# A hybrid encoder layer on one Trainium2 core: the first feed-forward product goes from eight block products to seven

## The chip, the core and the metric

The kernel runs on one core of one Trainium2 chip. Its time is the time of one execution in device microseconds; lower is better. Five engines work side by side, each on its own queue in order: PE (TensorE, the matrix products), DVE (VectorE), ACT (ScalarE), POOL (GpSimd) and SP (SyncE, which issues most DMA transfers). A profile names instructions by engine and by line of the kernel file; "L75 DVE" is a vector instruction that line 75 issued.

## The reference

The reference is one layer of a hybrid encoder over 512 tokens of 1024 features, in float32. A gated branch and an attention branch are mixed, multiplied by `w_out`, normalised and added to the input, which gives `h`. Then comes the feed-forward part:

```
mix_out = merged @ w_out
h = h + rms_norm(mix_out, norm_mix_post)
n2 = rms_norm(h, norm_mlp_pre)
hid = square(relu(n2 @ w_up))            # 512 x 1024 by 1024 x 4096
h = h + rms_norm(hid @ w_down, norm_mlp_post)
```

## The kernel before

All large products run on PE in a 32-bit format of reduced precision (`F32R`). To keep float32 accuracy each operand is split into a high part `hi` (a copy on ACT, L74 or L79) and the rest `lo` (a subtraction on DVE, L75 or L80), and each product is three matmuls: high times high, high times low, low times high (`mm3`, L82 to L86). So a product costs three matmuls with a 128x128 stationary tile and a moving tile of up to 512 columns.

The back half of the kernel, with which this case deals, has three stages.

- **`w_out` (L543 to L583).** Eight accumulators in PSUM, one for each token tile `t` (128 tokens) and half of the features, are filled over eight feature tiles `k`. The first four `k` go over all tokens; the last four (`last`, L563) are done token tile by token tile, so that one token tile ends 24 matmuls after the other. When a token tile is complete, `post_norm` (L529) takes ACT Squares of the PSUM banks (L534, into a scratch tile `junk`), multiplies by the gain on DVE (L538), computes the reciprocal root on DVE and POOL (`rstd_of`, L90, L93, L96) and adds the residual (L541). The tile `h2`, all four token tiles in one buffer, was loaded with x by one POOL DMA. Then a second norm follows: Squares of `h2` on ACT (L574, into a second `junk`), `rstd_of` again, the scaled tile `xn` on DVE (L578), eight PE transposes (L581) and the split into `n2h` and `n2l` (L583). `xn` has a single buffer.
- **`w_up` (L587 to L623).** `KF` is 32: there are 32 tiles of 128 hidden features, in 16 loaded pairs of 1 MB. The first four tiles (`NSPLIT`) are computed in two halves of 256 tokens, first tokens 0 to 255 of all four, then 256 to 511, because the second half of the tokens is normalised later. The other 28 tiles take all 512 tokens in one go: 24 matmuls of 512 columns each. `up_evac` (L601) makes relu on ACT (L604) and the product with the PSUM tile on DVE (L605), which is the square of relu. All 32 `hid` tiles stay in SBUF.
- **`w_down` (L627 to L659).** For each of the 32 hidden tiles the weights and `hid` are split, and 24 matmuls of 512 columns go into eight accumulators; the last four hidden tiles are done token tile by token tile, with `post_norm` and the output DMA behind each. `dpool`, which holds the split `hid` tiles, is opened before the pools of the `w_up` stage.

The order of the instructions in each engine's queue is set when the kernel is built: a scheduler runs a timing model of the program and writes out the queues. At run time an engine waits on semaphores at the head of its queue and nothing overtakes.

Of the kernel before, what the change touches and what calls it, by code (L numbers as in the profile page):

```python
# [10 lines left out]
F32 = mybir.dt.float32  # L11
F32R = mybir.dt.float32r
AF = mybir.ActivationFunctionType
# [23 lines left out]
def block_kernel(ctx: ExitStack, tc: tile.TileContext, x, norm_mix_pre, w_in, b_gate, ln_v_gain, ln_v_bias,  # L37
# [14 lines left out]
    wpool = pool(ctx, "wpool", bufs=3)  # L52

    ident = consts.tile([P, P], F32, name="ident")
    cols = consts.tile([P, 24], F32, name="cols")
# [366 lines left out]
    rows = gpool.tile([24, P], F32, name="rows")  # L422
    for i, (vec, n) in enumerate(((b_gate, 16), (ln_v_gain, 4), (ln_v_bias, 4))):
        o = (0, 16, 20)[i]
        nc.gpsimd.dma_start(rows[o:o + n], vec[0].rearrange("(a p) -> a p", p=P))
    wsp = gpool.tile([P, 4, P], F32, name="wsp")
    nc.gpsimd.dma_start(wsp, w_spatial.rearrange("g t s -> t g s"))
    pt = psA.tile([P, 24], F32, name="ptr", tag="T")
    nc.tensor.transpose(pt, rows, ident[:24, :24])
# [84 lines left out]
    hpool = pool(back, "hpool", side="right")  # L514
    gain2 = hpool.tile([P, 3, D], F32, name="gain2")
    for i, gn in enumerate((norm_mix_post, norm_mlp_pre, norm_mlp_post)):
        nc.gpsimd.dma_start(gain2[:, i], gn.to_broadcast([P, D]))
    h2 = hpool.tile([P, 4, D], F32, name="h2")
    nc.gpsimd.dma_start(h2, x.rearrange("(t p) d -> p t d", p=P))
    n2s = ExitStack()  # L520
    n2pool = pool(n2s, "n2pool", side="right")
    n2h = n2pool.tile([P, KD, S], F32R, name="n2h")
    n2l = n2pool.tile([P, KD, S], F32R, name="n2l")
    halves = [slice(0, 512), slice(512, 1024)]

# [3 lines left out]
    def post_norm(pss, gain, yp, dst, res):  # L529
        ss = small.tile([P, 2], F32, name="ss2")  # L530
        ys = []
        for hf, hs in enumerate(halves):
            junk = yp.tile([P, 512], F32, name="junk", bufs=1)
            nc.scalar.activation(junk, pss[hf], AF.Square, accum_out=ss[:, hf:hf + 1])  # L534
# [29 lines left out]
    ypool = pool(wo, "ypool")  # L564
    for t in range(4):
        ts_ = slice(t * P, (t + 1) * P)
        for hf in range(2):
            for k, wh, wl in last:
                w_out_mm(t, k, hf, wh, wl)
        post_norm(accs[t], gain2[:, 0], ypool, h2[:, t], h2[:, t])  # L570
        ss = small.tile([P, 2], F32, name="ss")
        for hf, hs in enumerate(halves):
            junk = ypool.tile([P, 512], F32, name="junk", bufs=1)
            nc.scalar.activation(junk, h2[:, t, hs], AF.Square, accum_out=ss[:, hf:hf + 1])  # L574
        r = rstd_of(ss, 1.0 / D)
        xn = ypool.tile([P, D], F32, name="xn2")
# [124 lines left out]
```

## Time and profile before

| | us |
|---|---|
| median of 3 runs | 842.18 |
| lowest and highest run | 841.86, 842.89 |
| the profiled execution's own time | 842.03 |
| its span in the profile | 840.2 |

| stage, by PE in the profiled execution | starts at, us |
|---|---|
| `w_out` | 435.95 |
| `w_up`, four tiles in halves | 481.30 |
| `w_up`, 28 tiles of 512 tokens | 506.02 |
| `w_down` | 659.84 |
| last matmul ends | 834.1 |

A timeline row of the profile is: start in us from the start of the span, duration in us, engine, line, operation, output<-inputs, shape, count; in brackets the idle time of the engine before it and what ended it. Matmuls are pipelined, so their durations overlap: the rate is read from the distance of their starts. A group row ends with total busy us and the mean ns of one.

### The profile page before, as it was taken

The numbers are of one execution on the slowest core, as the hardware profiler recorded it, in microseconds if no ns is written. First come the engines' busy times: TensorE is split into PE (matmuls) and PEld (weight loads), VectorE is DVE, ScalarE is ACT, GpSimd is POOL, SyncE is SP. The second block draws the span as 40 slices with busy tenths as digits, with TensorE's granted clock in tenths as the row PEclk, the third lists the DMA queues.
The fourth block names the chain that finished last, engine by engine and source line by source line (L and its number), as shares of the span: only waits on it lengthen the run. The fifth ranks groups of instructions, "written<-read, shape, count | busy, mean of one in ns | idle before, by whom it ended". The sixth has DMA issues, their size and how long they took to land. (4 is left out here: it accounts for less than half of the span.)

```text
span 840.2 us, 9719 instructions
## 1 busy us (share of the span) xinstructions
PE 826.9 (98%) x3867; PEld 693.9 (83%) x3867; DVE 419.4 (50%) x711; ACT 293.3 (35%) x479; POOL 74.9 (9%) x67
## 2 busy tenths in 40 slices
PE   7999999999999999999999999999999999999997
PEld 5899888888888778888888898888888888888885
DVE  6422788878874647433334744333333433333425
ACT  6322243435344353333233533222222322333312
POOL 2000123232214200000010100000000000000001
PEclk9999999999999999999999999999999999999999
DMA  9433233323114131431457103333323132222202
GB/s 306 129 101 88 68 96 101 84 67 96 56 52 125 51 100 62 140 101 50 151 195 236 44 2 101 100 101 101 101 100 101 53 131 86 87 98 99 101 1 100
DMA packets 69278, 83.14 MB, mean 99 GB/s; under 512 B 1849, under 2 KB 57297, under 8 KB 69234
## 3 DMA queue, kind: packets, MB, share of 16 engines
q1 hardware_dynamic: 67810, 77.67, 29.3%
q0 software_dynamic: 1424, 4.87, 1.7%
q8 instruction: 30, 0.49, 0.2%
q14 instruction: 14, 0.11, 0.0%
HBM read 80.43 MB, written 2.10 MB: 98 GB/s over the span
## 5 line engine op out<-in xcount | busy, mean ns | idle before, releaser
L84 PE MATMUL pf<-nh,hi 128*128 128x512 f32 x352 | 138.7, 394 | 0.6 <-DVE u L445 0.6
L86 PE MATMUL pf<-nh,lo 128*128 128x512 f32 x352 | 139.3, 396 | 0.0
L85 PE MATMUL pf<-nl,hi 128*128 128x512 f32 x352 | 138.1, 392 | 0.0
L85 PE MATMUL pu<-n2l,hi 128*128 128x512 f32 (+1 forms) x288 | 105.9, 369 | 0.1
L84 PE MATMUL pu<-n2h,hi 128*128 128x512 f32 (+1 forms) x288 | 105.1, 368 | 0.0
L86 PE MATMUL pu<-n2h,lo 128*128 128x512 f32 (+1 forms) x288 | 104.5, 364 | 0.0
L85 PE MATMUL pd<-lo,hh 128*128 128x512 f32 x256 | 99.6, 389 | 0.0
L84 PE MATMUL pd<-hi,hh 128*128 128x512 f32 x256 | 99.3, 389 | 0.0
L86 PE MATMUL pd<-hi,hl 128*128 128x512 f32 x256 | 98.6, 389 | 0.0
L75 DVE TENSOR_TENSOR lo<-upw,hi 128x1024 fp32r<-128x1024 f32 x32 | 39.1, 1225 | 103.0 <-ACT hi L74 103.0
L84 PEld LDWEIGHTS pf<-nh,hi 128*128 128x128 f32 x352 | 66.2, 188 | 14.3 <-DVE u L445 0.9
L86 PEld LDWEIGHTS pf<-nh,lo 128*128 128x128 f32 x352 | 66.2, 188 | 14.3 <-issue 0.2
L85 PEld LDWEIGHTS pf<-nl,hi 128*128 128x128 f32 x352 | 66.2, 188 | 14.1
L74 ACT ACTIVATE hi<-upw 128x1024 fp32r<-128x1024 f32 x32 | 33.8, 1060 | 111.7 <-PE pu L85 100.6
L80 DVE TENSOR_TENSOR hl<-hid,hh 128x512 fp32r<-128x512 f32 x32 | 21.9, 691 | 80.6 <-ACT hh L79 80.6
L84 PEld LDWEIGHTS pu<-n2h,hi 128*128 128x128 f32 x288 | 53.8, 188 | 9.9
L86 PEld LDWEIGHTS pu<-n2h,lo 128*128 128x128 f32 x288 | 54.0, 188 | 9.4
L85 PEld LDWEIGHTS pu<-n2l,hi 128*128 128x128 f32 x288 | 54.1, 188 | 8.6 <-DVE n2l L80 0.3
L247 POOL TENSOR_TENSOR sw<-sw,rope 32x512 f32<-32x512 f32 x24 | 42.4, 1767 | 176.8 <-DVE sw L245 159.6
L84 PEld LDWEIGHTS pd<-hi,hh 128*128 128x128 f32 x256 | 48.0, 188 | 10.1
L85 PEld LDWEIGHTS pd<-lo,hh 128*128 128x128 f32 x256 | 48.0, 188 | 10.1
L86 PEld LDWEIGHTS pd<-hi,hl 128*128 128x128 f32 x256 | 48.0, 188 | 9.8
(201 smaller groups left out, 1306.2 us busy)
## 6 DMA issues: line engine op xcount, KB each, us to landing
upw<-in_w_up_dram SPq DMA_DIRECT2D x16, 1024.0 KB, 5.5
dnw<-in_w_down_dram SPq DMA_DIRECT2D x16, 1024.0 KB, 4.8
qkw<-in_w_in_dram SPq DMA_DIRECT2D x24, 512.0 KB, 4.7
gw<-in_w_in_dram SPq DMA_DIRECT2D x8, 1024.0 KB, 5.3
slab<-in_w_in_dram SPq DMA_DIRECT2D x6, 1024.0 KB, 12.8
wow<-in_w_out_dram SPq DMA_DIRECT2D x4, 1024.0 KB, 4.9
w0raw<-in_w_in_dram SPq DMA_DIRECT2D x4, 512.0 KB, 7.0
uw<-in_w_in_dram SPq DMA_DIRECT2D x2, 1024.0 KB, 5.1
```

What stands on the lines that cost most here:

```text
L74: nc.scalar.activation(hi, raw, AF.Copy)
L75: (sub or nc.vector).tensor_tensor(lo, raw, hi.bitcast(F32), op=ALU.subtract)
L80: nc.vector.tensor_tensor(lo, src, hi.bitcast(F32), op=ALU.subtract)
L84: nc.tensor.matmul(ps, ah, bh, start=start, stop=False)
L85: nc.tensor.matmul(ps, ah, bl, start=False, stop=False)
L86: nc.tensor.matmul(ps, al, bh, start=False, stop=stop)
L247: nc.gpsimd.tensor_tensor(sw, sw, rope[:, 1], op=ALU.mult)
```

## The change

The product of `n2` (tokens by features) and `w_up` is done, for the last 14 of the 16 pairs of hidden tiles, as a 2x2 block product with seven block products in place of eight. The blocks are: tokens 0 to 255 and 256 to 511; even and odd feature tiles (`k` even, `k` odd); the first and the second hidden tile of the pair. One block product runs over four feature tiles with three matmuls each, on 256 tokens: 12 matmuls of 256 columns; a pair takes 84 of them.

- **Sums of activations.** `n2` is kept in float32 (`n2f`) as well as split (`nb`, four blocks). Four block sums are formed in place in `n2f` on DVE and split into four more blocks `nt`, once.
- **Sums of weights.** For each pair `prep` forms four block sums of the raw weights on DVE (tile `s`), and splits seven blocks of weights (`s12`, `s34`, and `a3` with three unchanged blocks).
- **Sums of results.** The products accumulate into three half banks `Y`, `Z`, `X` of PSUM, which are continued from product to product; in between ACT and DVE copy intermediate values to SBUF (`p1`, `z5`, `u2`, `u3`) and put the four result blocks together. Product 4 of a pair (`tail`) stands in the code behind product 6 of the next one. Relu and square are then two ACT passes over both hidden tiles in place.
- **Space.** The added tiles take SBUF. `h2` is therefore no longer kept: x is loaded per token tile (two buffers), the sum goes out to a DRAM tile `h2d` and is loaded again for the last norm. `wpool` is closed after `w_out` and another opened; `dpool` is opened only after the `w_up` stage's pools are closed. `post_norm` gets its scratch from its caller: in the `w_out` stage that is `xn2`, the one buffer of the scaled tile, and at the end the output tile `o`. The gain of the second norm is no longer a row over all partitions but a column (`gcol`), applied after the transposes (L592), and the scaling by the root moves from DVE to ACT (L588).

```diff
+    n2pool = pool(back, "n2pool", bufs=14, side="right")
+    hpool = pool(rst, "hpool", bufs=2, side="right")
...
-            junk = yp.tile([P, 512], F32, name="junk", bufs=1)
-            nc.scalar.activation(junk, pss[hf], AF.Square, accum_out=ss[:, hf:hf + 1])
+            nc.scalar.activation(junk[:, hs], pss[hf], AF.Square, accum_out=ss[:, hf:hf + 1])
...
     for t in range(4):
+        h2 = hpool.tile([P, D], F32, name="h2")
+        nc.gpsimd.dma_start(h2, x[ts_])
         for hf in range(2):
             for k, wh, wl in last:
                 w_out_mm(t, k, hf, wh, wl)
-        post_norm(accs[t], gain2[:, 0], ypool, h2[:, t], h2[:, t])
+        xn = ypool.tile([P, D], F32, name="xn2")
+        post_norm(accs[t], gain, ypool, h2, h2, xn)
+        nc.gpsimd.dma_start(h2d[ts_], h2)
         ss = small.tile([P, 2], F32, name="ss")
         for hf, hs in enumerate(halves):
-            junk = ypool.tile([P, 512], F32, name="junk", bufs=1)
-            nc.scalar.activation(junk, h2[:, t, hs], AF.Square, accum_out=ss[:, hf:hf + 1])
+            nc.scalar.activation(xn[:, hs], h2[:, hs], AF.Square, accum_out=ss[:, hf:hf + 1])
         r = rstd_of(ss, 1.0 / D)
-        xn = ypool.tile([P, D], F32, name="xn2")
         for q, hs in enumerate(halves):
-            nc.vector.scalar_tensor_tensor(xn[:, hs], h2[:, t, hs], r, gain2[:, 1, hs], op0=ALU.mult, op1=ALU.mult)
+            nc.scalar.activation(xn[:, hs], h2[:, hs], AF.Copy, scale=r)
...
-            split_into(n2h[:, ks, ts_], n2l[:, ks, ts_], pt)
+            nc.vector.tensor_tensor(n2f[:, 4 * q:4 * q + 4, ts_], pt, gcol[...], op=ALU.mult)
+        for kh in range(2):
+            hi, lo = nb[kh, t // 2]
+            o = slice(t % 2 * P, t % 2 * P + P)
+            split_into(hi[:, :, o], lo[:, :, o], n2f[:, kh:KD:2, ts_])
...
+    for nm, src in ((2, fo[:, :, B]), (1, fe[:, :, A]), (3, fe[:, :, B]), (4, fo[:, :, A])):
+        nt[nm] = (n2_tile(), n2_tile())
+        split_into(*nt[nm], src)
...
+    def prep(i):
+        raw = raw_up(i).rearrange("p (j h) (r c) -> p j (h r) c", h=2, r=2)
+        s = upool.tile([P, KH, 4, P], F32, name="s", bufs=1)
+        nc.vector.tensor_tensor(s[:, :, 0:4:2], raw[:, :, 1:3], raw[:, :, 0:1].to_broadcast([P, KH, 2, P]), op=ALU.add)
+        nc.vector.tensor_tensor(s[:, :, 3], s[:, :, 2], raw[:, :, 1], op=ALU.add)
+        s12 = wsplit(s[:, :, 2:4])
+        a3 = [z.rearrange("p (j m c) -> p j m c", m=3, c=P) for z in a3_tiles()]
+        split_into(*a3, raw[:, :, 1:4])
+        nc.vector.tensor_tensor(s[:, :, 1], s[:, :, 3], raw[:, :, 3], op=ALU.add)
+        s34 = wsplit(s[:, :, 0:2])
...
+    def product(n, ps, w, first):
+        (wh, wl), (bh, bl) = w[n], moving[n]
+        for j in range(KH):
+            for m, (a, b) in enumerate(((wh, bh), (wh, bl), (wl, bh))):
+                nc.tensor.matmul(ps, a[:, j], b[:, j], ...)
...
+    for i in range(NSTD, KF // 2):
+        w = prep(i)
+        Y, Z, X = half_bank("acc"), half_bank("acc"), half_bank("tp")
+        product(6, Y, w, True)
+        if tail:
+            tail()
+        product(1, X, w, True)
+        nc.scalar.activation(p1, X, AF.Copy)
+        nc.vector.tensor_tensor(u2, Y, p1, op=ALU.add)
+        product(5, Z, w, True)
+        nc.scalar.activation(z5, Z, AF.Copy)
+        product(2, X, w, False)
+        nc.scalar.activation(c1[:, :256], X, AF.Copy)
+        product(7, Y, w, False)
+        nc.vector.scalar_tensor_tensor(u3, Y, -1.0, p1, op0=ALU.mult, op1=ALU.subtract)
+        product(3, Z, w, False)
+        nc.vector.tensor_tensor(c1[:, 256:], Z, u2, op=ALU.add)
+        nc.vector.tensor_tensor(c2[:, 256:], u3, z5, op=ALU.subtract)
+
+        def tail(w=w, Y=Y, p1=p1, c2=c2, f=f):
+            product(4, Y, w, False)
+            nc.vector.scalar_tensor_tensor(c2[:, :256], Y, -1.0, p1, op0=ALU.mult, op1=ALU.subtract)
+            both = hid[f // 8][:, f % 8:f % 8 + 2]
+            nc.scalar.activation(both, both, AF.Relu)
+            nc.scalar.activation(both, both, AF.Square)
+    tail()
+    up.close()
...
+    dpool = pool(dn, "dpool", bufs=2)
```

The scheduler writes the queues anew, and at three places they differ in a way on which the prediction rests. In the rows below the lines of the changed kernel are its own, one higher than before in the helpers.

The PE queue before, where `w_out` goes over into `w_up` (`pd` is an accumulator of `w_out`, `pt` a bank of transposes, `xn` the scaled token tile, `pu` an accumulator of `w_up`); the transposes are those of token tile 1:

```order
L84 MATMUL pd<-hi,mh 128x512
L85 MATMUL pd<-lo,mh 128x512
L86 MATMUL pd<-hi,ml 128x512
L581 MATMUL pt_3753<-ident,xn_3751 128x128 x4
L581 MATMUL pt_3761<-ident,xn_3751 128x128 x4
L84 MATMUL pd<-hi,mh 128x512
L85 MATMUL pd<-lo,mh 128x512
L86 MATMUL pd<-hi,ml 128x512
L84 MATMUL pu<-n2h,hi 128x256 x2
L85 MATMUL pu<-n2l,hi 128x256
```

Behind the last matmul of `w_out` the first halves of `w_up` follow at once, and the transposes of token tiles 2 and 3 stand 24 and 87 rows further down, among matmuls of `w_up`. The same place in the PE queue of the changed kernel:

```order
L85 MATMUL pd<-hi,mh 128x512
L86 MATMUL pd<-lo,mh 128x512
L87 MATMUL pd<-hi,ml 128x512
L591 MATMUL pt_3763<-ident,xn_3736 128x128 x4
L591 MATMUL pt_3770<-ident,xn_3736 128x128 x4
L591 MATMUL pt_3833<-ident,xn_3806 128x128 x4
L591 MATMUL pt_3840<-ident,xn_3806 128x128 x4
L591 MATMUL pt_3903<-ident,xn_3876 128x128 x4
L591 MATMUL pt_3910<-ident,xn_3876 128x128 x4
L85 MATMUL pu<-n_3483,a_3937 128x256
L86 MATMUL pu<-n_3484,a_3937 128x256
```

All transposes of token tiles 1, 2 and 3 now stand ahead of the first matmul of `w_up`. Those of token tile 0 stand 19 `w_out` matmuls ahead of the end of `w_out`.

The ACT queue of the changed kernel at the same place (`xn_3736`, `xn_3806` and so on are the token tiles' turns in the one buffer `xn2`, `n_` the split blocks `nb`, `a_3937` the high part of the first hidden tile's weights):

```order
L588 ACTIVATE xn_3666<-h_3640,rs_out 128x512 x2
L541 ACTIVATE xn_3736,ss_3737<-pd 128x512 x2
L80 ACTIVATE n_3483<-n2f 128x4x128
L80 ACTIVATE n_3485<-n2f 128x4x128
L585 ACTIVATE xn_3736,ss<-h_3710 128x512 x2
L588 ACTIVATE xn_3736<-h_3710,rs_out 128x512 x2
L541 ACTIVATE xn_3806,ss_3807<-pd 128x512 x2
L80 ACTIVATE n_3483<-n2f 128x4x128
```

Before, the first Squares (L534) wrote to `junk`. Now they write to `xn`, the buffer that the transposes of the token tile before read.

The ACT queue of the changed kernel where `w_up` goes over into `w_down` (`hid` is the hidden tile, `hh` the split of the first one for `w_down`, `dnw` its weights):

```order
L705 ACTIVATE hid<-ptp 128x256
L80 ACTIVATE hhl<-hid 128x512 x2
L75 ACTIVATE hi<-dnw 128x1024
L716 ACTIVATE hid<-hid 128x1024
L80 ACTIVATE hh<-hid 128x512 x2
```

The first split `hh` stands behind the relu (L716) of the last pair. Before, the two first splits `hh` stood among the first relus of `w_up`.

More of the change, by code (lines that the diff above doesn't have):

```diff
@@ L427, in block_kernel @@
     nc.gpsimd.dma_start(wsp, w_spatial.rearrange("g t s -> t g s"))
[L428 to L429 removed]
+    pt = psA.tile([P, 32], F32, name="ptr", tag="T")
+    nc.tensor.transpose(pt, rows, ident[:32, :32])
     nc.vector.tensor_copy(cols, pt)
```

157 lines of the change are left out of this document (99 added, 58 removed).

## The prediction

> **What bounds the kernel now.** I read the page's busy times first, then PE's waits, then the timeline at the stage borders.
>
> ```profile
> span 840.2 us, 9719 instructions
> PE 826.9 (98%) x3867; PEld 693.9 (83%) x3867; DVE 419.4 (50%) x711; ACT 293.3 (35%) x479; POOL 74.9 (9%) x67
> PE pgn L148 <- DMA grow<-in_norm_mix_pre_dram: 2.3, 1, 2.3
> PE pf L84 <- ACT hi L74: 1.2, 1, 1.2
> ```
>
> PE is busy for 98% of the span, and the longest of its waits after the start is 1.2 us. So the kernel is as long as its matmuls, one behind the other, and a change acts in two ways: by the array time that it takes out, and by any wait that it puts into PE's queue. The rate of the matmuls and the stage borders stand in the timeline:
>
> ```profile
> 435.95 0.40 PE L84 MATMUL pd<-hi,mh 128*128 128x512 f32 x1
> 481.07 0.39 PE L86 MATMUL pd<-hi,ml 128*128 128x512 f32 x1
> 481.30 0.39 PE L84 MATMUL pu<-n2h,hi 128*128 128x256 f32 x2
> 504.02 0.28 PE L85 MATMUL pu<-n2l,hi 128*128 128x256 f32 x1
> 505.90 0.28 PE L86 MATMUL pu<-n2h,lo 128*128 128x256 f32 x1
> 506.02 0.39 PE L84 MATMUL pu<-n2h,hi 128*128 128x512 f32 x1
> 659.84 0.39 PE L84 MATMUL pd<-hi,hh 128*128 128x512 f32 x1
> ```
>
> The 28 full tiles of w_up are 672 matmuls of 512 columns from 506.02 to 659.84: 0.2289 us each. Of 256 columns, 16 steps lie between 504.02 and 505.90: 0.1175 us each. That is 2.6% more than half; the price of the narrow matmul, weight load included, is small. w_out runs from 435.95 to 481.30 without a wait.
>
> **The array time taken out.** A pair now costs 48 x 0.2289 = 10.99 us. Changed, it costs 84 x 0.1175 = 9.87 us. The gain is 1.12 us for each of 14 pairs: **-15.6 us**. It holds only if DVE and ACT can feed a pair within 9.87 us:
>
> ```profile
> L75 DVE TENSOR_TENSOR lo<-upw,hi 128x1024 fp32r<-128x1024 f32 x32 | 39.1, 1225 | 103.0 <-ACT hi L74 103.0
> L80 DVE TENSOR_TENSOR hl<-hid,hh 128x512 fp32r<-128x512 f32 x32 | 21.9, 691 | 80.6 <-ACT hh L79 80.6
> L605 DVE TENSOR_TENSOR hid<-pu,relu 128x512 f32<-128x512 f32 x32 | 21.9, 683 | 4.5 <-ACT relu L604 4.5
> L74 ACT ACTIVATE hi<-upw 128x1024 fp32r<-128x1024 f32 x32 | 33.8, 1060 | 111.7 <-PE pu L85 100.6
> ```
>
> On DVE a pair has three passes of 1024 elements (1.23 us each), two of 512 (0.69), one of 1536 (1.23 plus the step of 0.53 from 512 to 1024, so 1.76) and five of 256 (0.68 less half that step, 0.42): 3.68 + 1.38 + 1.76 + 2.08 = 8.9 us, where it had 3.8. On ACT there are four passes of 1024, one of 1536 and three of 256, at 1.06, about 1.5 and 0.4: 6.9 us. Both stay under 9.87, DVE by 1.0 us, and consecutive vector operations overlap by 0.09 us each (the pair of rows 483.62 and 484.21 below), which makes the margin about 2 us. I take no stall in the steady pairs; the bound on the other side is a rival below. The four block sums of n2 and their splits (eight passes of 1024 on DVE, 9.8 us) and the first pairs' weights lie beside the 22.6 us of the four tiles in halves; DVE has some 21 us of work there, so this cover is thin, and 1 to 2 us would show if it failed.
>
> **The wait put in.** The queues in the section on the change say that PE now has the transposes of token tiles 1, 2 and 3 ahead of the first w_up matmul, and that the first Squares of a token tile go to the buffer that the transposes of the tile before read. So one tile's chain can't begin before the other's ends, and PE, which has nothing else left in front of it, waits for them in turn. The links of a chain, from rows of the same operations:
>
> ```profile
> 460.68 0.60 ACT L534 ACTIVATE junk<-pd 128x512 f32<-128x512 f32 x1 [1.66 <-PE pd L86]
> 461.40 0.69 DVE L538 TENSOR_TENSOR y<-pd,gain 128x512 f32<-128x512 f32 x1 [1.12 <-ACT junk L534]
> 471.02 1.41 DVE L541 SCALAR_TENSOR_TENSOR h<-y,rs_out,h 128x512 f32<-128x512 f32 x2
> 471.87 0.63 ACT L574 ACTIVATE junk<-h 128x512 f32<-128x512 f32 x1 [2.28 <-DVE h L541]
> 472.63 0.63 ACT L574 ACTIVATE junk<-h 128x512 f32<-128x512 f32 x1
> 473.38 0.16 DVE L93 SCALAR_TENSOR_TENSOR rs_in<-ss,rs_in 128x1 f32<-128x1 f32 x1 [0.60 <-ACT junk L574]
> 473.63 1.03 PE L581 MATMUL pt<-ident,xn 128*128 128x128 f32 x8
> 473.69 0.55 POOL L96 TENSOR_TENSOR rs_out<-rs_in,neghalf 128x1 f32<-128x1 f32 x1 [2.70 <-DVE rs_in L93]
> 474.27 1.09 ACT L79 ACTIVATE n2h<-pt 128x512 fp32r<-128x512 f32 x2 [0.20 <-PE pt L581]
> 474.42 0.48 PE L85 MATMUL pd<-lo,mh 128*128 128x512 f32 x1
> 483.62 0.68 DVE L80 TENSOR_TENSOR n2l<-pt,n2h 128x512 fp32r<-128x512 f32 x1
> 484.21 0.68 DVE L538 TENSOR_TENSOR y<-pd,gain 128x512 f32<-128x512 f32 x1
> ```
>
> Counted from a tile's first Square: the second Square starts at 0.76 (471.87 to 472.63); the second y 0.72 after it (460.68 to 461.40), at 1.48; rs_in queues behind that y for 0.59 (483.62 to 484.21), at 2.07; POOL starts 0.31 later and takes 0.55, done at 2.93. On DVE the two lo splits of the tile before stand ahead of h, 0.59 each from 2.2, so h starts at 3.4. The Square of h follows 0.85 after (4.25), the second 0.76 later (5.01), rs_in 0.75 later (5.76), POOL until 6.62, the first scaled copy on ACT 0.63 more, and the transposes start at 7.3. The second copy is 0.5 behind, so the last transpose is done at 8.4, and the next tile's Square may start. **A tile costs 8.4 us.**
>
> When does the first chain start? The 192 w_out matmuls take (481.30 - 435.95 - 2 x 0.79) / 192 = 0.228 us each (0.79 is 473.63 to 474.42, eight transposes). Tile 0's transposes stand behind 173 of them, at 475.4; they land at 476.4, and w_out ends at 480.5. Tile 1's transposes are then due at 483.75, tile 2's at 492.15, tile 3's at 500.55. Behind them the high part of the first hidden tile's weights (1.06 on ACT) is due at 502.1. There w_up starts; 192 x 0.1175 = 22.6 us later, at 524.7, the block products start, where 506.02 stood before: **+18.6 us**. Before, these chains ran beside 22.6 us of half tiles; that cover now lies behind them.
>
> The x loads and h2 stores on POOL's queue are passed in the same stretch. The load for tile 3 must wait until tile 1's store has landed, and stands ahead of tile 2's rs_out. Transfers of that size on that queue:
>
> ```profile
> gain<-in_norm_mix_post_dram POOLq DMA_DIRECT2D x1, 512.0 KB, 4.8
> gain<-in_norm_mlp_post_dram POOLq DMA_DIRECT2D x1, 512.0 KB, 6.2
> h<-in_x_dram POOLq DMA_DIRECT2D x1, 2048.0 KB, 11.2
> ```
>
> Tile 1's h is written at 481.1. With a landing of 4.8 to 6.2 the load is issued by 486 to 487.3, just ahead of tile 2's rs_out at 487.2; I count 0, and at most some 0.7 us. The row of 2048 KB is the bound for a slow one, a rival.
>
> **The border to w_down.** The first hh stands behind the last pair's relu on ACT, since its buffer lies where w_up's tiles lay. After the last matmul DVE finishes a lo of w_down weights that it has just begun (up to 1.1), makes the last 256-wide block (0.42), ACT the relu of 1024 (1.06) and the first hh of 512 (0.63): **+3.0 us**, between 2.1 without the lo and 3.3. Before, w_down followed in step.
>
> **The clock after the wait.** PE stands still for 3.2, then 7.2 and 7.3 us. What its clock does then is seen at the two ends of the profile:
>
> ```profile
> 7.26 1.97 PE L167 MATMUL pt<-ident,xn 128*128 128x128 f32 x8 [1.17 <-DVE xn L164]
> 10.78 0.63 PE L85 MATMUL pv<-lo,nh 128*128 128x512 f32 x1
> 15.05 0.47 PE L86 MATMUL pv<-hi,nl 128*128 128x512 f32 x1
> 834.00:835.00 1.00, 0.09 (x1) 0.00 (x0) 0.09 (x2) 0.69 (x2) 0.00 (x0) 1.00 0.00 0
> 836.00:837.00 1.00, 0.00 (x0) 0.00 (x0) 1.00 (x2) 0.00 (x0) 0.00 (x0) 1.00 0.00 0
> 837.00:838.00 1.00, 0.00 (x0) 0.00 (x0) 0.21 (x1) 0.00 (x0) 0.00 (x0) 0.90 0.59 219
> 838.00:839.00 1.00, 0.00 (x0) 0.00 (x0) 0.00 (x0) 0.00 (x0) 0.00 (x0) 0.50 0.81 305
> ```
>
> The granted clock (third number from the right) goes to 0.50 about 3.8 us after the last matmul at 834.1. From 10.78 to 15.05 ten matmuls took 0.427 us each, nearly double, and only then came the full rate; eight transposes took 1.97 us against 1.03. So tiles 2 and 3 find a half clock. Eight cold transposes end 1.97 us after the first one's start instead of 1.1: 0.87 for tile 2, and for tile 3 0.4, because the weights are due only at 502.1. Then w_up starts cold: some 4.3 to 5 us as from 10.19 or 10.78 to 15.05, at 0.2135 in place of 0.1175, which loses 45% of 5 us, 2.2. Together **+3.5 us**, with 1.5 and 5 as its ends.
>
> The Trainium skill's page "TensorE: Matmul & The Clock Gate", Part 1, says that the array falls to half rate after an idle window of about 3.4 us and returns after about 3.4 us of sustained work, in windows that run freely. By that page the cold start would be 3.4 to 6.8 us long, an estimate of 1.5 to 3.1 us, and neither pause of 3.2 or 3.0 us alone would close the gate; the trace's 3.8 us agrees with it.
>
> **The sum.** Against the profiled execution's own 842.03 us (its span and 1.8 us around it; the median of the runs is 842.18): -15.6 + 18.6 + 3.0 + 3.5 = +9.5. The kernel gets slower, **851.5 us**. DVE's rate, the signals between engines (each link of the chain 0.03 to 0.1) and POOL's transfers add more easily than they take away.
>
> **The rivals.**
>
> 1. The gate stays open, or closes for less than a microsecond's worth. 842.03 - 15.6 + 18.6 + 3.0 = 848.0. For it: the eight transposes fall between the pauses. Against it: two pauses of 7 us are twice what closed it at the end. 0.12.
> 2. The chains overlap as they did and PE waits little, so the array time decides: 842.03 - 15.6 + 3.0 = 829.4, faster. The point from which it decides: the wait must come under 9 us with a cold start, 12 without. For it: before, the same chains ran beside matmuls and cost nothing. Against it: the rows of both queues and the single buffer. 0.06.
> 3. DVE becomes the bound of the pairs. If each of the two splits of sums lets DVE wait for its ACT pass (1.06 us, since DVE's queue keeps order), a pair costs 8.9 + 2.1 = 11.0 us instead of 9.87, and the gain is gone: 851.5 + 14 x 1.1 = 867. For it: 103 us of DVE's idle time before L75 is exactly that wait. Against it: the queue places other DVE work between. 0.05.
> 4. POOL's 512 KB transfers land as late as the 2048 KB one, after 11.2 us. Tile 3's x load is then issued at 492.3, which holds back tile 2's rs_out by 5 us, and lands at 503.5, which tile 3's h (due 496.6 plus these 5) meets 2 us late: 858. For it: stores and loads share the stage with 1 MB weight loads. Against it: 512 KB rows say 4.8 to 6.2. 0.06.
>
> **How the numbers follow.** The forecast holds 0.71. From the clock's ends and 0.5 to 1 for signals it reaches from 849 to 854.5. The range takes in rival 1 and half of rival 4: 847.5 to 857; rivals 2 and 3 and the rest of 4, 0.14, are left out. Of 0.06 for rival 2 a part of 0.01 ends within 0.2% (1.7 us, about what a measurement of this kernel can tell from no change), and 0.01 of the forecast's lower side too: faster 0.05, same 0.02, slower 0.93.
>
> **What would show it.** PE's waits should name the transposes of L591 with some 18 us in three pieces of about 3, 8 and 8 us; the time from w_out's last matmul to the first w_up matmul should be about 22 us. The granted clock should be 0.5 in the last of these and in the first microseconds of w_up. The pairs should start 9.9 us apart, with DVE busy for 80 to 90% of them. The first w_down matmul should wait some 3 us for ACT's hh. If the pairs are 11 us apart, rival 3 holds; if POOL shows issues waiting for a store ahead of rs_out, rival 4; if w_up starts by 490, rival 2 and my reading of the queue is wrong.

## The result and the profile after

The changed kernel takes 857.35 us in the median of four runs (856.65 to 858.22), against 842.18 us: 1.0179 times as long, with a 95% interval of 1.0162 to 1.0197. The forecast was 851.5 us, in a range from 847.5 to 857. The direction was right, the size was not: +15.2 us where +9.3 was said. In the profiled executions the span grows by 14.7 us, from 840.2 to 854.9. One execution of the first shifted kernel below, the profiled one, ran in a slower state (1032.08 us at a granted clock of 0.755), so the figure given for that kernel is the median of its other three and it has no counts.

The head of the page of the changed kernel, and two rows of its list of PE's waits (microseconds in all, times, longest):

```profile
span 854.9 us, 10911 instructions
PE 821.1 (96%) x4371; PEld 709.0 (83%) x4371; DVE 492.2 (58%) x817; ACT 347.6 (41%) x547; POOL 82.5 (10%) x78
PE pt L591 <- ACT xn L588: 17.6, 3, 7.3
PE pd L85 <- ACT hh L80: 2.9, 1, 2.9
```

PE is busy for 5.8 us less, and stands for 20.5 us in two waits that the kernel before did not have. Both are the ones named in the prediction. The stage borders, from PE's timeline of the changed kernel: the first matmuls of the front's feature products (`pf`), of w_out, of w_up, of the block products and of w_down.

```profile
84.20 0.40 PE L85 MATMUL pf<-nh,hi 128*128 128x512 f32 x1
440.46 0.39 PE L85 MATMUL pd<-hi,mh 128*128 128x512 f32 x1
508.18 0.56 PE L85 MATMUL pu<-n,a 128*128 128x256 f32 x1
532.17 0.39 PE L679 MATMUL pacc<-n,hi 128*128 128x256 f32 x2
672.45 0.79 PE L85 MATMUL pd<-hi,hh 128*128 128x512 f32 x1 [2.92 <-ACT hh L80]
```

In the kernel before, PE's timeline has the first `pf` matmul here:

```profile
83.34 0.40 PE L84 MATMUL pf<-nh,hi 128*128 128x512 f32 x1
```

From these borders and those of the prediction, in us (the prediction's column follows from its stations, with the cold transposes and the cold start of w_up counted where they lie):

| stretch | before | predicted | after | after less predicted |
|---|---|---|---|---|
| start to w_out's first matmul | 435.95 | 435.95 | 440.46 | +4.5 |
| from there to w_up's first matmul | 45.35 | 67.4 | 67.72 | +0.3 |
| from there to w_down's first matmul | 178.54 | 166.0 | 164.27 | -1.7 |
| from there to the end | 180.36 | 180.36 | 182.45 | +2.1 |
| span | 840.2 | 849.7 | 854.9 | +5.2 |

The two stretches that the change works on came out 1.4 us better than forecast. The two that the prediction left as they were came out 6.6 us worse, and the miss of 5.2 us is what remains. The experiments are about the larger of these first.

### The profile page after: what moved, and what is told of

Its sections match the earlier page's. It is cut to its first block, busy times and chain, and to the rows that moved or that the text cites. A ratio compares the mean times of both kernels' runs of the same rounds, so it can differ in the third digit from the quotient of the medians.

```text
span 854.9 us, 10911 instructions
## 1 busy us (share of the span) xinstructions
PE 821.1 (96%) x4371; PEld 709.0 (83%) x4371; DVE 492.2 (58%) x817; ACT 347.6 (41%) x547; POOL 82.5 (10%) x78
## 4 chain that ended last, share of the span: by engine, by line
PE 94%; ACT 2%; DVE 1%; DMA 1%; issue 1%; SPq 0%; POOL 0%; DVEq 0%; POOLq 0%; ACTq 0%
PE pf L87 11%; PE pf L86 11%; PE pf L85 11%; PE pacc L679 11%; PE pd L85 8%; PE pd L86 8%; PE pd L87 8%; PE ptp L679 5%; PE pv L85 4%; PE pv L87 4%; PE pv L86 4%; PE pu L85 1%; PE pu L86 1%; PE pu L87 1%; PE py L407 1%
## 5 line engine op out<-in xcount | busy, mean ns | idle before, releaser
L86 PE MATMUL pd<-lo,hh 128*128 128x512 f32 x224 | 87.9, 392 | 0.0
L87 PE MATMUL pd<-hi,hl 128*128 128x512 f32 x224 | 86.0, 389 | 0.0
L679 PE MATMUL pacc<-n,hi 128*128 128x256 f32 x448 | 80.9, 279 | 0.0
L86 PEld LDWEIGHTS pf<-nl,hi 128*128 128x128 f32 x352 | 66.1, 188 | 15.2
L679 PEld LDWEIGHTS pacc<-n,hi 128*128 128x128 f32 x448 | 68.4, 188 | 0.0
L679 PE MATMUL pacc<-n,lo 128*128 128x256 f32 x224 | 61.3, 279 | 0.0
L80 ACT ACTIVATE hh<-hid 128x512 fp32r<-128x512 f32 x28 | 17.6, 631 | 97.4 <-PE pd L86 97.4
L85 PE MATMUL pv<-hi,nh 128*128 128x512 f32 x128 | 52.1, 411 | 1.5 <-ACT nh L80 1.5
L87 PE MATMUL pv<-hi,nl 128*128 128x512 f32 x128 | 51.9, 407 | 0.0
L86 PE MATMUL pv<-lo,nh 128*128 128x512 f32 x128 | 51.9, 405 | 0.0
L76 DVE TENSOR_TENSOR lo<-dnw,hi 128x1024 fp32r<-128x1024 f32 x32 | 39.2, 1225 | 17.7 <-ACT hi L75 17.7
```

What stands on the lines that cost most here:

```text
L76: (sub or nc.vector).tensor_tensor(lo, raw, hi.bitcast(F32), op=ALU.subtract)
L80: nc.scalar.activation(hi, src, AF.Copy)
L85: nc.tensor.matmul(ps, ah, bh, start=start, stop=False)
L86: nc.tensor.matmul(ps, ah, bl, start=False, stop=False)
L87: nc.tensor.matmul(ps, al, bh, start=False, stop=stop)
L679: nc.tensor.matmul(ps, a[:, j], b[:, j], start=first and not (j or m), stop=(j == KH - 1 and m == 2), skip_group_check=True)
```

## Experiments on the front: where the tiles lie

The front runs the same matmuls in both kernels. The page shows those on the features a little slower in the mean (397 ns for `pf` in place of 392 to 396), and a count shows it better, over 80 us in the middle of the `pf` stage, in which PE never waits. This is the table of stretches of the kernel before, the same stretch 330 to 410, and its stretch 700 to 800 in w_down; behind the times stand PE's busy time and the number of its matmuls, then PEld, DVE, ACT, POOL, the granted clock, the DMA share and GB/s.

```profile
330.00:410.00 80.00, 80.00 (x351) 65.66 (x350) 33.09 (x44) 26.75 (x37) 0.00 (x0) 1.00 0.32 106
700.00:800.00 100.00, 100.00 (x443) 82.81 (x442) 36.51 (x38) 29.54 (x37) 0.00 (x0) 1.00 0.28 95
```

The same two stretches of the changed kernel:

```profile
330.00:410.00 80.00, 80.00 (x345) 64.26 (x344) 32.38 (x43) 25.25 (x35) 0.00 (x0) 1.00 0.30 97
700.00:800.00 100.00, 100.00 (x443) 82.84 (x442) 34.89 (x37) 29.50 (x38) 0.00 (x0) 1.00 0.28 95
```

The clock is 1.00 in all four, w_down has its 443 matmuls in both, and `pf` has 345 in place of 351: 1.7% slower, at a full clock and with no wait. What the change does touch there is the tile `cols` in the constants, which grows from 24 to 32 columns. Whatever is allocated behind it on the left side of the on-chip memory (the weights' `hi` and `lo`, the stationary operand) then lies 32 bytes further on, and the tiles on the right side (`nh` and `nl`, the moving operand) stay. In w_down, up to its last four hidden tiles, both operands lie on the left and move together.

Three kernels tried this first, with the width of `cols` as the only edit. Two of them are the kernel before:

```
-    cols = consts.tile([P, 24], F32, name="cols")
+    cols = consts.tile([P, 32], F32, name="cols")    # e1; [P, 40] in e2
...
-    nc.vector.tensor_copy(cols, pt)
+    nc.vector.tensor_copy(cols[:, :24], pt)
```

> The kernel before, with the tile of per-column constants 32 columns wide in place of 24, its first 24 used as before: no work changes, only the tiles allocated behind it on the same side of the on-chip memory lie 32 bytes further on, as in the changed kernel, while the tiles allocated from the other side stay. Theory A (the matrix engine reads a little slower when its two operands lie 32 bytes apart within 64): the stages up to w_out take about 3.5 to 4.5 us longer, as they do in the changed kernel (w_out started at 440.46 there, at 435.95 before), the pf matmuls are 0.233 us apart in the mean in place of 0.2295, the up stage slows too, and the time is about 846 to 847. Theory B (the 4.5 us come from something else in the changed program, such as instructions in another order or an ordinary variation): no change, 842.2 within 0.5.

> The same with 40 columns: the tiles lie 64 bytes further on, so that the phase of the two operands within 64 bytes is that of the kernel before. Theory A: no change, 842.2 within 0.5. A theory by which any shift or any other program makes the stages slower: 845 to 847, as for the shift by 32 bytes.

The shift by 32 bytes alone made the kernel before 850.52 us, 1.0096 times its time (1.0079 to 1.0113), and the shift by 64 bytes made it 837.29, 0.9948 times (0.9932 to 0.9965). So the place of the tiles moves the unchanged kernel by +8.5 and -4.8 us. The first is some 4 us more than expected, and no trace shows in which stage. Theory B falls, theory A holds in its direction, and its period of 64 bytes is wrong. The changed kernel with 40 columns:

> The changed kernel, with the tile of constants 40 columns wide in place of 32, so that the tiles behind it have the phase of the kernel before again. Theory A: w_out starts at about 436.5, the matmuls on the last four hidden tiles are 0.227 us apart in place of 0.233, and the time is 4 to 5 us less, 852.5 to 853.5, which is the sum of the prediction with its clock terms as measured. Theory B: 857.3 within 0.5.

It took 849.51 us, 7.8 less, where 4 to 5 were expected. Its `pf` stage is 348.71 us long where it was 356.26. The block products got slower, 144.1 in place of 140.3 us: a placement that suits the matmuls of 512 columns does not suit those of 256.

I then thought of a period of 128 bytes, and tried 56 columns in both kernels. (The expectations call the block products Strassen products.)

> The kernel before with the tile of constants 56 columns wide, which puts the tiles behind it 128 bytes further on than in the kernel before. The runs with 32 and 64 bytes gave +8.6 and -4.75 us, so that a period of 64 bytes is out. Theory A2 (what counts is the distance of the two operands of a matmul within 128 bytes; with 512 columns 0.2267 us apart at a distance of 0, 0.2295 at 64, 0.2333 at 32): the kernel before has its distance of 64 in the front again, and the time is 842.0 within 0.7, with w_out's start within 0.7 of 435.95. If the period is longer than 128 bytes or the place itself counts: a time between 835 and 851 other than that.

> The changed kernel with the tile of constants 56 columns wide: its front tiles then lie 128 bytes further on than in the kernel before, which by theory A2 is the same placement, so that this run against the kernel before is the change without the shift. Theory A2: the front's pf stage takes 352.6 us as before in place of 356.3, w_up starts at about 503.5, the Strassen stage takes 140 to 142 us, w_down's 175 us, and the time is 852 to 854 against 842.1, that is 10 to 12 us above, where the prediction had 9.3. Rival (the front's slowness belongs to the changed program, not to its addresses): 856.5 to 858.

The kernel before took 849.56 us, 7.5 more, and its `pf` stage 356.85 us: theory A2 falls too. (The changed kernel took 851.41 us with its `pf` stage at 356.01: its block products had become faster, 136.4 us.) But the counts in the traces so far fitted one rule, theory D: what counts is the address of the moving operand less that of the stationary one, with its sign, modulo 256 bytes. The traces hold no addresses, but the built kernels do: `nh` lies at 192480; a slot of `hi` lies at 44704 before and at 44736 after, which makes 64 and 32. Two runs tested the rule: a shift by 256 bytes, and the other side moved by 32 bytes.

```
-    cols = consts.tile([P, 24], F32, name="cols")
+    cols = consts.tile([P, 88], F32, name="cols")    # e14
```

> The kernel before with 88 columns of constants, 256 bytes more on the left side. Theory D (period 256): the time of the kernel before, 842.0 within 0.7, with a pf stage of 352.6 us. If the period is longer, or what counts is not the place: another value of those seen at 32, 64 and 128 bytes, 837 to 851.

```
     right = ExitStack()
+    pool(right, "padpool", side="right").tile([P, 8], F32, name="pad")    # e15
     npool = pool(right, "npool", side="right")
```

> The kernel before with its 24 columns, and 32 unused bytes at the outer end of the right side while the front runs, so that the normed tokens (moving operand of pf and pv) lie 32 bytes lower and the left side does not move. Theory D: the pf stage's distance becomes +32 in place of +64, three pf matmuls take 0.700 us in place of 0.6884, the pf stage takes 356.3 us in place of 352.6, and the time is 845.5 to 846.5; the stages from w_out on, whose tiles lie where they lay, keep their times within 0.5 us. Rival (the place on the left counts, or the code): 842.0 within 0.7.

With 256 bytes the kernel before took 841.91 us, 1.0000 times its time (0.9990 to 1.0009). With the right side moved it took 847.18, 0.7 us above what I expected, and its stages from w_out on kept their lengths within 0.1 us. Its `pf` stage is 357.21 us long, 4.6 more than before. The stretch 330 to 410 of this last kernel, whose left side lies where it lay:

```profile
330.00:410.00 80.00, 80.00 (x345) 64.26 (x344) 32.02 (x42) 25.13 (x35) 0.00 (x0) 1.00 0.29 93
```

It has 345 matmuls, as the changed kernel has. So it is the distance of the operands, not the place on the left, that slows the front. The last hidden tiles of w_down say the same with the sides exchanged: in the changed kernels their stationary operand lies on the right and their moving one on the left, and, counted in the same way, their matmuls come 0.2333 us apart at a distance of -32, 0.2267 at 0 and 0.2289 at +64. Matmuls counted in stretches without a wait, by distance (moving less stationary, modulo 256 bytes):

| distance | 512 columns, `pf`, in 80 us | 512 columns, w_up of before, in 60 us | 256 columns, block products, in 60 us |
|---|---|---|---|
| 0 | 354 to 355 | 267 | 502 |
| +64 | 351 to 352 | 263 to 264 | 512 |
| +32 | 344 to 345 | not counted | 516 to 517 |
| -64 | 345 | 259 | 532 |

The last run of this row shows what the change costs without the shift: the changed kernel with 88 columns, so that its tiles have the placement of the kernel before.

> The changed kernel with 88 columns of constants: its left side then lies 256 bytes further on than in the kernel before, a shift that left the time of the kernel before where it was (841.9 against 842.1), so that this is the change with the placement of before. Theory D: the pf stage takes 352.6 us in place of 356.3; the Strassen products, now at a distance of +64, are 0.1178 us apart in place of 0.1166, so that their stage takes 141.5 in place of 140.3; the waits stay as they were; the time is about 854.5 to 855.5, the change itself 12.5 to 13.5 us, of which the prediction had 9.3. If the change's slower front had a part that is not placement: 856.5 or more.

It took 851.96 us beside 842.35 for the kernel before on the same chip: +9.6 us, 1.0117 times (1.0100 to 1.0134). I had expected 3 us more. Three things in its trace make the difference: the `pf` stage was 351.66 us, 0.9 below that of before, whose trace has a wait of 0.6 us on `u` there that the changed kernels don't have; w_down's stretch was 181.1 us in place of 182.4 of the changed kernel, which the section on the handover explains; and `pf` began at 83.32 in place of 84.20 of the changed kernel. The stretch 330 to 410 of this kernel:

```profile
330.00:410.00 80.00, 80.00 (x351) 65.66 (x350) 33.93 (x44) 26.88 (x37) 0.00 (x0) 1.00 0.32 106
```

The 351 matmuls are back. Its span is 849.7 us, which is the prediction's 840.2 + 9.5; but part of this agreement is luck, since its front is 1.0 us shorter than forecast and its w_down 0.7 us longer. The change costs 9.6 us where its tiles lie as before, and the changed kernel as it stands takes 5.4 us more than that (857.35 - 851.96). In the two profiled executions these are 5.2 us: +4.6 in the `pf` stage, -1.6 in w_up and the block products, which like the distance of +32 better than +64, +0.9 at the start and +1.3 at the start of w_down. The first two, 3.0 us together, are placement. The start differs as much between changed kernels of one placement, and the next sections show what the 1.3 us hang on.

## Experiments on the wait between w_out and w_up

PE's transposes in the changed kernel, from its timeline, with the wait ahead of each group in brackets:

```profile
479.70 1.03 PE L591 MATMUL pt<-ident,xn 128*128 128x128 f32 x8
488.03 1.97 PE L591 MATMUL pt<-ident,xn 128*128 128x128 f32 x8 [2.97 <-ACT xn L588]
497.30 1.97 PE L591 MATMUL pt<-ident,xn 128*128 128x128 f32 x8 [7.30 <-ACT xn L588]
506.56 1.97 PE L591 MATMUL pt<-ident,xn 128*128 128x128 f32 x8 [7.30 <-ACT xn L588]
```

The tiles come 9.27 and 9.26 us apart, the forecast's 8.4 and 0.87 for cold transposes. That the one buffer `xn2` sets this was argued from the queues; a buffer of its own for the squares that are thrown away tests it.

```
+    junk = n2pool.tile([P, D], F32, name="junk2", tag="n2")
...
-        post_norm(accs[t], gain, ypool, h2, h2, xn)
+        post_norm(accs[t], gain, ypool, h2, h2, junk)
...
-            nc.scalar.activation(xn[:, hs], h2[:, hs], AF.Square, ...)
+            nc.scalar.activation(junk[:, hs], h2[:, hs], AF.Square, ...)
```

> The changed kernel, with a buffer of its own for the squares that the two row norms throw away, in place of the buffer of the normed rows. Theory of the prediction (the wait between w_out and w_up comes from one token tile's squares being kept behind the other tile's transposes by the one buffer): the four chains overlap, the transposes of tiles 1 to 3 come closer than 9.3 us to each other, the distance from w_out's start to w_up's falls from 67.7 us to 56 to 60, and the time to about 846 to 850. Rival (the distance is the work of the vector engines itself, or the stores and loads of h2): the distance stays above 65 us and the time above 855.

It took 843.09 us, 14.3 less than the changed kernel and hardly more than the kernel before (1.0015 times, 1.0005 to 1.0024). From w_out's first matmul to w_up's there are 55.74 us in place of 67.72, which is 12.0 of the 13.1 us between the two profiled executions; 1.5 more are its earlier `pf` stage (82.67 in place of 84.20), whose instructions are the same, and 0.4 are lost behind w_up's start. The rival falls. The same rows of this kernel's timeline:

```profile
478.65 1.03 PE L592 MATMUL pt<-ident,xn 128*128 128x128 f32 x8
483.43 1.03 PE L592 MATMUL pt<-ident,xn 128*128 128x128 f32 x8
485.56 1.27 PE L592 MATMUL pt<-ident,xn 128*128 128x128 f32 x8 [1.09 <-ACT xn L589]
493.06 1.97 PE L592 MATMUL pt<-ident,xn 128*128 128x128 f32 x8 [6.24 <-ACT xn L589]
```

The first three tiles now come within 7 us. Before the last one PE still stands 6.24 us, with matmuls of w_up for the finished tiles behind it in its queue. Which place in the queue the transposes get hangs on the a3 buffer: as long as the first early hidden tile needs it, and it lies where the norm's tiles lay, w_up can't be placed ahead. Beside the own buffer the next kernel gives it to the last early tile; in this run alone that hidden tile was computed with the weights of the one before it, the same work on other numbers.

```
-            if i == 0 and j == 0:
+            if i == NSTD - 1 and j == 1:
                 wh, wl = (... for z in a3_tiles())
```

> The changed kernel with a buffer of its own for the squares (which gave 843.1) and, beside it, the a3 tile for the last of the eight hidden tiles that come early in place of the first, so that the order of the program may put matmuls of w_up ahead of the transposes of the late token tiles. Where the rest of the wait is PE's queue (with the own buffer PE still stood 6.2 us before the transposes of tile 3 while w_up matmuls of other tiles lay behind them): w_out's start to w_up's falls below 50 us in place of 55.7, part of it comes back as waits inside w_up, and the time is 839 to 842. Where the rest of the wait is the vector engines' work itself: 843 within 1.

It took 840.88 us, 2.2 less again. From w_out to w_up there are 47.83 us. Of the 7.9 us gained there in the profiled executions 3.6 come back inside w_up, whose stretch to w_down grows from 164.55 to 168.18. PE's timeline of this kernel, from tile 2 on:

```profile
486.44 1.27 PE L592 MATMUL pt<-ident,xn 128*128 128x128 f32 x8 [1.22 <-ACT xn L589]
488.69 0.39 PE L86 MATMUL pu<-n,hi 128*128 128x256 f32 x1 [0.49 <-DVE n L81]
491.21 0.38 PE L86 MATMUL pu<-n,hi 128*128 128x256 f32 x1 [1.20 <-DVE n L81]
496.22 0.60 PE L592 MATMUL pt<-ident,xn 128*128 128x128 f32 x4
501.69 0.39 PE L87 MATMUL pu<-n,a 128*128 128x256 f32 x1 [1.48 <-DVE a L81]
```

The transposes of tile 3 now come at 496.22 without a wait, among matmuls of w_up, and what is left are pauses of 0.5 to 1.5 us on DVE's splits.

## Experiment on the handover to w_down, and the clock

The start of w_down in the changed kernel's timeline, and the stretch around it with its granted clock (third number from the right):

```profile
672.45 0.79 PE L85 MATMUL pd<-hi,hh 128*128 128x512 f32 x1 [2.92 <-ACT hh L80]
673.04 0.63 PE L86 MATMUL pd<-lo,hh 128*128 128x512 f32 x1
674.75 0.63 PE L86 MATMUL pd<-lo,hh 128*128 128x512 f32 x1
675.48 0.40 PE L86 MATMUL pd<-lo,hh 128*128 128x512 f32 x1
```

```profile
672.00:676.00 4.00, 3.55 (x10) 2.84 (x11) 2.59 (x4) 3.01 (x5) 0.00 (x0) 0.59 0.66 266
```

The wait on `hh` is the 3 us that were forecast. Behind it the matmuls are 0.43 us apart until 675.2 (four of them from 673.04 to 674.75), and the clock of the stretch is 0.59: it fell to half within this pause, which is called here that the clock gate closed. One kernel mends the handover alone.

```
+    prepool = pool(dn, "prepool")                  # opened ahead of w_up's pools
+    hh0 = prepool.tile([P, S], F32R, name="hh0")   # and hl0
...
+        if i == KF // 2 - 2:
+            split_into(hh0, hl0, hid_of(0))
...
-        nc.scalar.activation(r, ps, AF.Relu)
-        nc.vector.tensor_tensor(hid_of(f), ps, r, op=ALU.mult)
+        nc.scalar.activation(hid_of(f), ps, AF.Relu)
+        nc.vector.tensor_tensor(hid_of(f), ps, hid_of(f), op=ALU.mult)
```

> The changed kernel with the handover to w_down alone mended: the split of hidden tile 0 gets buffers of its own that are opened ahead of w_up's and is made before the end of the pair loop, and the relu is written into the hidden tile, so that the matmuls of w_down's first column tile are not behind the last pair's relu. The wait of 2.9 us on hh goes. If the slow matmuls at the start of w_down (0.43 us apart for some 3 us) come from the wait having closed the clock gate, they go with it and the time is 4.3 to 4.7 us less, 852.6 to 853.1; if the prediction's reading held, that a pause of 3 us closes nothing, the slow start has another cause, stays, and the time is 2.9 us less, 854.4.

It took 854.18 us, 3.2 less, but its runs spread from 851.51 to 855.23, so the time does not tell the two readings apart. Its trace has no slow start (the clock is 1.00 throughout 655 to 676), and from w_up's first matmul to the end there are 343.2 us in place of 346.7: 2.9 us for the wait and 1.3 for the closed gate went, and a new wait of 0.7 us on a later `hh` came. Such a pause does not always close the gate. This is the start of w_down in the changed kernel with the placement of before (88 columns):

```profile
668.59 0.50 PE L85 MATMUL pd<-hi,hh 128*128 128x512 f32 x1 [2.89 <-ACT hh L80]
668.92 0.39 PE L86 MATMUL pd<-lo,hh 128*128 128x512 f32 x1
669.15 0.40 PE L85 MATMUL pd<-hi,hh 128*128 128x512 f32 x1
```

Here 2.89 us of standing closed nothing: the second matmul follows 0.33 us after the first, and then 0.23. That is 1.3 us between its stretch of 181.11 us from w_down's start and the 182.45 of the other.

What decides is not the 0.03 us between the two pauses but how each falls on a grid. Within every trace of this case the granted clock changes only at times that are a whole number of 3.413 us apart; in the changed kernel these are 487.59, 511.48, 671.91 and 675.32, which are 7, 47 and 1 such steps. These are the step of the grid in which the changed kernel stands, and the one behind it:

```profile
668.50:671.91 3.41, 1.03 (x9) 0.82 (x8) 2.23 (x4) 1.70 (x3) 0.00 (x0) 1.00 1.00 363
671.91:675.32 3.41, 2.87 (x7) 2.29 (x8) 2.06 (x4) 3.10 (x5) 0.00 (x0) 0.50 0.79 317
```

The same two steps of the kernel with 88 columns, whose pause lies across the border of a step:

```profile
666.77:670.18 3.41, 1.59 (x7) 1.33 (x8) 1.38 (x3) 3.19 (x5) 0.00 (x0) 1.00 1.01 401
670.18:673.59 3.41, 3.41 (x17) 2.83 (x16) 1.29 (x2) 1.64 (x3) 0.00 (x0) 1.00 0.21 87
```

With PE busy for 1.03 us of the step the clock fell at its end, with 1.59 us it did not. In the 14 traces at a full clock every step with at most 1.42 us of busy PE ended with the fall, and every one with at least 1.59 us without it. Of the six changed kernels that have this pause, of 2.86 to 3.00 us, four closed the gate and two did not, so the 1.3 us are a matter of luck. This is read from the traces; no run moved a pause on purpose.

At the wait between w_out and w_up, the stretches of the changed kernel are plain:

```profile
484.00:488.00 4.00, 1.06 (x5) 0.56 (x3) 1.81 (x5) 2.14 (x6) 1.14 (x2) 0.95 0.28 111
488.00:510.00 22.00, 7.38 (x32) 6.58 (x33) 13.41 (x27) 13.54 (x29) 4.59 (x7) 0.50 0.20 76
510.00:512.00 2.00, 2.00 (x14) 2.00 (x13) 2.00 (x3) 0.48 (x1) 0.00 (x0) 0.63 0.00 0
```

The clock is at 0.50 from 487.59, within the first pause, of 2.97 us, and stays there through three groups of transposes until the matmuls of w_up, which start at 508.18, have run for some 3 us.

## A version that beats both

All three mends together, with 40 columns of constants:

```
    cols [P, 40]; own buffer junk2; a3 for the last early hidden tile,
    split from raw[:, :, P:]; hh0 and hl0 ahead of w_up
```

> The changed kernel with all three mends and 40 columns of constants: own buffer for the squares (-14.3 alone), a3 for the last early hidden tile (with the own buffer another -2.2), the handover to w_down (-3.2 alone), and the shift by 64 bytes (-7.8 alone). If the four are independent: 857.35 - 14.3 - 2.2 - 3.2 - 7.8 = 829.9, that is 828.5 to 831.5, below the kernel before (842.2) and below the kernel before with the same shift (837.3). If they cover one another (the shift makes the matmuls with 256 columns slower, 0.120 us apart in place of 0.1166, and what one wait gives back another takes): 832 to 837.

It took 834.21 us, 0.9910 times the kernel before (0.9893 to 0.9926): the second case, in which the gains cover one another. The last kernel adds 64 unused bytes that bring the block products from a distance of 0 to one of -64.

```
+    pool(back, "padpool", side="right").tile([P, 16], F32, name="pad")
     n2pool = pool(back, "n2pool", bufs=14, side="right")
```

> The same with 64 unused bytes ahead of the pool that holds the normed and transposed tokens, on the right side, so that the moving operand of w_up and of the Strassen products lies 64 bytes below the phase of its stationary operand (modulo 256), where it had the same phase. Theory D (the time of three matmuls goes by the distance of moving and stationary operand within 256 bytes; with 256 columns 0.360 us at 0, 0.3535 at +64, 0.350 at +32, 0.341 to 0.343 at -64; with 512 columns 0.680 at 0, 0.687 at +64, 0.700 at +32, -32 and -64): the Strassen stage takes 136.5 us in place of 144, the last four hidden tiles 0.687/0.680 of their 22 us, and the time is 6.5 to 8 us below the run without these 64 bytes. Rival (the left side's place alone counts): no difference.

It took **825.10 us, 0.9798 times the kernel before** (0.9783 to 0.9812), 9.1 us below the one without the 64 bytes, where 6.5 to 8 were expected; the two profiled executions are 7.8 us apart. The stretch 560 to 620 of the kernel without them, within the block products:

```profile
560.00:620.00 60.00, 60.00 (x502) 60.00 (x501) 50.04 (x65) 37.48 (x49) 0.00 (x0) 1.00 0.39 115
```

The same stretch with them:

```profile
560.00:620.00 60.00, 60.00 (x532) 60.00 (x531) 52.53 (x70) 38.39 (x49) 0.00 (x0) 1.00 0.37 107
```

There are 532 matmuls in place of 502, and DVE is busy for 88% of the stretch and does not hold PE up in it. Part of this is placement, which the old scheme can have as well: with 64 bytes it took 837.29. Against that, the fastest placement of the old scheme that was tried, the scheme of seven products with its waits taken out is worth 12.2 us.

## Why the prediction was wrong, and where it was right

**The wait put in, +18.6, and its cold transposes: right.** The pauses were 2.97, 7.30 and 7.30 us where 3.2, 7.2 and 7.3 were worked out, w_out to w_up took 67.72 us where 67.4 was due, and the run with a buffer for the squares shows that the single buffer is the cause. POOL's transfers, counted at 0, held nothing up: PE's wait rows name only the scaled copy, and in POOL's queue every `rs_out` of the stage starts when DVE's `rs_in` releases it. Rival 2 had the right mechanism, but for another kernel: with a buffer more the chains do overlap in large part, and the time is 843.1, about that of before and not the rival's 829.4.

**The array time, -15.6, and the handover, +3.0: right.** Together they were -12.6 us, from the first block product to w_down 153.82 - 12.6 = 141.2 us; the changed kernel took 140.28 (532.17 to 672.45), and 141.56 in the placement of before. The wait on `hh` was 2.9. Rival 3 is out: this is the stretch 560 to 620 of the changed kernel, where DVE is busy for 87% of the time (80 to 90% were named) and PE never waits.

```profile
560.00:620.00 60.00, 60.00 (x516) 60.00 (x516) 52.19 (x71) 38.76 (x50) 0.00 (x0) 1.00 0.34 104
```

**The clock, +3.5: nearly right in size, wrong in one sentence.** The cold start of w_up lasted 3.1 us (the matmuls are 0.213 us apart from 508.54 to 511.31) and not 4.3 to 5, which made it 0.8 us cheaper. That neither pause of 3.2 or 3.0 us alone would close the gate did not hold: after 2.97 us it had closed, after 2.92 us it had closed and cost 1.3 us at w_down's start, after 2.89 us in another kernel it had not. The Trainium skill's page "TensorE: Matmul & The Clock Gate", Part 1, from which that sentence came, has idle windows of about 3.4 us that run freely. The steps of 3.413 us agree with it; what differs is that a step need not be idle throughout, since one with 1.42 us of busy PE still closed the gate, and there the measurement decides.

**The sum: here it failed.** "-15.6 + 18.6 + 3.0 + 3.5" has no term for the front and for the body of w_down, where the matmuls stay as they are. But the diff widens `cols` by 32 bytes, and the `pf` matmuls came 1.7% slower by it: 4.6 us for the stage, by the run with the placement of before. Against the kernel before the stage is 3.65 us longer, because the changed program is 0.95 us shorter there, 0.6 of it the wait on `u`. Some 0.9 us more of the front's 4.5 is the later start of the `pf` stage (84.20 in place of 83.34), within what it differs by between changed kernels of the same placement (82.67 to 84.20). Of the 2.1 us behind w_down's start 1.3 are the closed gate, which the prediction had ruled out there, and some 0.6 are the 96 products of the last four hidden tiles, whose split (`hhl`) now lies on the right side, so that they come 0.233 us apart in place of 0.227. With its tiles placed as before the changed kernel takes 851.96 us beside the forecast's 851.5; there the gate stayed open at w_down, which it might not have done.

## What to carry to other kernels

Where a scratch output is folded into a live buffer, ask who still reads it: one buffer more was worth 14.3 us here, where the change had lost 15.2. A change that widens an early tile moves everything behind it; before a per cent is put down to the change, run the old kernel with the same shift, and count matmuls in a stretch without waits. And a sum of links, each from a row of the same operation, held to 2 us for the stretches that it covered. What it lacked was a look at what the diff moves without touching it.

## What the runs showed of the hardware

The rate of the matmuls depends on the distance of their two operands in memory, as far as the distances here were tried. With float32 split into high and low parts as here, at a full clock, 80 us hold 344 to 355 matmuls of 512 columns, and 60 us hold 502 to 532 of 256 columns; the best distance for the long ones (0 modulo 256 bytes) is the worst for the short ones. The same distances gave the same counts whichever side was moved, and a shift by 256 bytes changed nothing. The Trainium skill's page "TensorE: Matmul & The Clock Gate", Part 2, says that the array has two independent read ports, so that loading the next weights takes no read bandwidth from the running matmul; the counts here differ by 3% and 6% with the distance alone, which suggests that something is shared. That is an inference, and what it is the traces don't show: other distances than these four (and one of -32, at which the last hidden tiles ran 0.233 us apart) were not counted.

The granted clock changes on a grid of 3.413 us. It fell at the end of a step in which PE was busy for at most 1.42 us and stayed full behind one with at least 1.59 us, so that pauses of 2.9 us closed the gate or not by where they lay. A half clock, once there, lasted through groups of eight transposes 9 us apart.
